# The first MLP as Strassen block products, with its middle rows kept in HBM

## The chip, the core and the metric

The kernel runs on one core of one Trainium2 chip. The metric is the device time of one launch in microseconds. The five engines of the core are TensorE (PE, with its weight loads listed as PEld), VectorE (DVE), ScalarE (ACT), GpSimd (POOL) and SyncE (SP), which here only issues transfers.

## The reference, cut to what matters

The model is a decoder trunk of two layers over 1040 tokens (16 meta tokens and 1024 others) of width 1024. Layer 0 mixes tokens by a recurrence and by attention, layer 1 by retention. After each mixer stands an MLP with a hidden width of 4096, and after each of the four parts a layer norm over a residual sum. The change is in the MLP of layer 0 and in what stands around it:

```
mix = _even_mixer(h, ...)                                  # ends in a projection by ev_w_out
h = _layernorm(DN_ALPHA * h + mix, ln_mix_g[l], ln_mix_b[l])
f = jnp.square(jax.nn.relu(h @ mlp_w1[l])) @ mlp_w2[l]      # 1024 -> 4096 -> 1024
h = _layernorm(DN_ALPHA * h + f, ln_mlp_g[l], ln_mlp_b[l])
```

## The kernel before, in words

**Layout and precision.** Everything is held transposed: 128 features on the partitions, tokens along the free dimension, so the width of 1024 is 8 tiles. To keep the precision of float32, each operand is split into a rounded part (`hi`, made by ACT, `round`, L294) and a remainder (`lo`, made by DVE's subtraction, L288 for weights). A product of two such pairs takes three matmuls per 128 rows of contraction (`mm3`, L321 to L323): hi x hi, hi x lo, lo x hi.

**Slots.** SBUF is cut into 50 slots of 1040 float32 per partition. `self.free` is a deque of their numbers: `slot` takes from its left end, `drop` puts back at its right end. The number is thus fixed while the program is written out. A tile in a slot that was used before waits for every reader and writer of the earlier tile, transfers among them. PSUM's eight banks of 512 float32 per partition are handed out in rings of their own (`bank`): s0 to s3 with one bank each, t0 and t1 with two.

**Weights.** `plan` lists all weight units of 128 x 1024 in the order of use. `weight` hands out the next one, and `ahead` loads and splits those that follow, as long as slots are free beyond a reserve.

**The MLP.** `out_proj` multiplies the attention half of the mixer's output, in four chunks of tokens (272, 256, 256, 256), and adds into the residual `acc` (L907). The norm of a chunk is a generator, `layer_norm`, put on a list; `pump` writes out a few of its steps between the matmuls of the next chunk, `settle` the rest. It sums over the tiles on POOL (L393, L395), subtracts the mean and scales on DVE (L406, L442), and splits the result (L449, L450); L452 keeps the residual. `mlp` then takes the hidden width in 8 blocks of 4 tiles. Up: one unit of w1 by all of x, then relu, square and split (L921 to L924). Down: four units of w2 by the block's four hidden tiles, added into `acc` by DVE (L956). The first block and the last run in the four chunks, so that they overlap with the norms before and after; all others run in three spans of 348, 346 and 346 columns. Hidden rows stay in SBUF.

**Order.** The order of the program gives the priority. A list scheduler that works with its own estimate of durations fixes the order on each engine and each queue when the program is built; on the chip each engine then goes through its list in order and waits where something isn't ready.

## Time and profile before

| | us |
|---|---|
| median of 3 runs (2863.98 to 2865.64) | 2864.4 |
| span of the profiled execution, from first to last instruction | 2862.4 |
| PE busy | 2795.6 (98%) |
| PE weight loads busy | 2531.5 (88%) |
| DVE busy | 1342.0 (47%) |
| ACT busy | 972.1 (34%) |
| POOL busy | 329.0 (11%) |

The profile gives for the profiled execution its span; nothing else of that execution's own time is shown, and the median of the timed runs lies 2.0 us above the span. Consecutive matmuls overlap in the profile, since each is shown with its whole passage through the array. The distance from start to start is therefore the cost of one, and PE's busy share says little of its pace. The granted clock is shown as a share of full speed.

### The profile page before, as it was taken

How to read it: one execution, taken by the hardware profiler on the slowest of the kernel's cores; microseconds unless marked ns; L12 is line 12 of the kernel's file. 1: busy time of each engine (PE TensorE's matmuls, PEld its weight loads, DVE VectorE, ACT ScalarE, POOL GpSimd, SP SyncE). 2: the span in 40 equal slices, each digit the busy share in tenths (PEclk: the TensorE clock that was granted, in tenths of full speed). 3: DMA queues.
4: the chain of work that ended last, by engine and by line, in shares of the span. 5: the costliest groups of instructions: out<-in, count | busy, mean ns of one | idle time of the engine just before them, and what ended most of it. 6: DMA issues, size and time to landing. Idle time of an engine off the chain costs nothing.

```text
span 2862.4 us, 38749 instructions
## 1 busy us (share of the span) xinstructions
PE 2795.6 (98%) x16142; PEld 2531.5 (88%) x16142; DVE 1342.0 (47%) x2381; ACT 972.1 (34%) x1857; POOL 329.0 (11%) x431
## 2 busy tenths in 40 slices
PE   8999999999999999989999999999999999999997
PEld 8898899999999999978888888788998888888896
DVE  6677868532233323575534635354473222222335
ACT  3757733522332223232414224141244212222133
POOL 1024524200000000230000000012140000000012
PEclk9999999999999999999999999999999999999998
DMA  3220130110111111111301303043101111111111
GB/s 135 74 72 5 53 134 16 38 59 30 52 37 60 41 49 45 45 45 52 125 16 45 118 35 114 15 140 125 67 31 38 59 52 37 52 40 56 52 37 60
DMA packets 49359, 168.53 MB, mean 59 GB/s; under 512 B 5776, under 2 KB 9616, under 8 KB 49184
## 3 DMA queue, kind: packets, MB, share of 16 engines
q1 hardware_dynamic: 40320, 134.97, 13.6%
q0 software_dynamic: 8288, 28.96, 3.1%
q8 instruction: 126, 2.06, 0.3%
q10 hardware_dynamic: 576, 2.13, 0.2%
q14 instruction: 49, 0.40, 0.0%
HBM read 143.94 MB, written 18.91 MB: 57 GB/s over the span
## 4 chain that ended last, share of the span: by engine, by line
PE 92%; DVE 4%; ACT 2%; issue 1%; POOL 1%; DMA 1%; POOLq 0%; SPq 0%; ACTq 0%; DVEq 0%
PE p L321 29%; PE p L323 29%; PE p L322 29%; PE p L847 1%; PE p L1266 1%; PE p L1267 1%; PE p L1268 1%; PE p L871 1%; DVE s L442 1%; DVE s L450 1%; PE p L873 1%; ACT s L825 0%; DVE s L406 0%; DVE st L818 0%; DMA s<-in_xT 0%
## 5 line engine op out<-in xcount | busy, mean ns | idle before, releaser
L321 PE MATMUL p<-s,s 128*128 128x512 f32 (+6 forms) x4886 | 1653.5, 340 | 28.2 <-POOL s L369 7.0
L322 PE MATMUL p<-s,s 128*128 128x512 f32 (+6 forms) x4886 | 1649.4, 338 | 1.5 <-DVE s L372 1.5
L323 PE MATMUL p<-s,s 128*128 128x512 f32 (+6 forms) x4886 | 1642.7, 338 | 1.6 <-DVE s L450 1.6
L321 PEld LDWEIGHTS p<-s,s 128*128 128x128 f32 (+1 forms) x4886 | 918.1, 188 | 113.3 <-ACT s L825 9.2
L322 PEld LDWEIGHTS p<-s,s 128*128 128x128 f32 (+1 forms) x4886 | 919.7, 188 | 77.4 <-DVE s L372 2.5
L323 PEld LDWEIGHTS p<-s,s 128*128 128x128 f32 (+1 forms) x4886 | 918.5, 188 | 77.5 <-DVE s L450 2.0
L294 ACT CAST s<-s 128x1024 fp32r<-128x1024 f32 (+5 forms) x331 | 277.4, 855 | 811.9 <-PE p L322 351.6
L956 DVE TENSOR_TENSOR s<-s,p 128x348 f32<-128x348 f32 (+4 forms) x328 | 178.7, 547 | 486.3 <-PE p L323 485.8
L288 DVE TENSOR_TENSOR s<-s,s 128x1024 fp32r<-128x1024 f32 x212 | 258.9, 1227 | 160.1 <-ACT s L294 103.0
L924 DVE TENSOR_TENSOR s<-s,s 128x346 fp32r<-128x346 f32 (+3 forms) x172 | 95.4, 563 | 337.8 <-ACT s L923 337.8
L921 ACT ACTIVATE s<-p 128x346 f32<-128x346 f32 (+3 forms) x172 | 82.7, 490 | 401.7 <-PE p L323 279.2
L393 POOL TENSOR_TENSOR s<-s,s 128x256 f32<-128x256 f32 (+1 forms) x16 | 13.9, 868 | 1383.3 <-DVE s L956 1262.6
L922 ACT ACTIVATE s<-s 128x346 f32<-128x346 f32 (+3 forms) x172 | 90.2, 525 | 3.2
L923 ACT CAST s<-s 128x346 fp32r<-128x346 f32 (+3 forms) x172 | 86.7, 513 | 3.9
L395 POOL TENSOR_TENSOR s<-s,s 128x256 f32<-128x256 f32 (+1 forms) x95 | 74.0, 781 | 104.9 <-DVE s L956 54.1
L1120 DVE TENSOR_TENSOR s<-p,s 128x512 fp32r<-128x512 f32 x32 | 22.1, 691 | 117.7 <-ACT s L1119 117.7
L341 DVE TENSOR_TENSOR s<-s,s 128x512 fp32r<-128x512 f32 (+6 forms) x121 | 65.1, 571 | 22.4 <-ACT s L294 20.7
L829 POOL TENSOR_SCALAR s<-s,st 116x808 f32<-116x808 f32 (+7 forms) x72 | 56.6, 789 | 79.0 <-DVE st L828 65.3
L850 DVE TENSOR_TENSOR s<-p,s 116x464 fp32r<-116x464 f32 (+3 forms) x120 | 59.3, 513 | 7.0 <-ACT s L849 5.6
L408 ACT ACTIVATE s<-s 128x256 f32<-128x256 f32 (+1 forms) x64 | 22.8, 417 | 115.0 <-DVE s L406 115.0
L1119 ACT CAST s<-p 128x512 fp32r<-128x512 f32 x32 | 18.7, 585 | 125.8 <-PE p L323 125.8
L847 PE MATMUL p<-consts,s 116*116 116x116 f32 (+2 forms) x360 | 54.7, 271 | 6.3 <-DVE s L850 1.9
(203 smaller groups left out, 1871.3 us busy)
## 6 DMA issues: line engine op xcount, KB each, us to landing
s<-in_w SPq DMA_DIRECT2D x128, 512.0 KB, 3.3
y_scratch<-s POOLq DMA_DIRECT2D x24, 512.0 KB, 9.3
s<-y_scratch POOLq DMA_DIRECT2D x24, 512.0 KB, 5.6
s<-in_wv SPq DMA_DIRECT2D x16, 512.0 KB, 4.2
s<-in_wg SPq DMA_DIRECT2D x16, 512.0 KB, 3.3
s<-in_xT SPq DMA_DIRECT2D x12, 520.0 KB, 5.6
s<-in_win SPq DMA_DIRECT2D x11, 512.0 KB, 8.7
s<-in_wout SPq DMA_DIRECT2D x8, 512.0 KB, 4.5
```

What stands on the lines that cost most here:

```text
L288: (self.nc.gpsimd if self.pool_lo else self.nc.vector).tensor_sub(lo[:, :n], s[:, :n], hi.f[:, :n])
L294: self.nc.scalar.copy(out, in_)
L321: self.nc.tensor.matmul(ps, wh, xh, start=(i == 0), stop=False)
L322: self.nc.tensor.matmul(ps, wh, xl, start=False, stop=False)
L323: self.nc.tensor.matmul(ps, wl, xh, start=False, stop=(stop and i == n - 1))
L395: (nc.vector if end and m == KT - 1 else nc.gpsimd).tensor_add(s1, s1, acc[m][:, cols])
L847: nc.tensor.transpose(tp[:n, c, :r], ps[q][:r, a:b], self.ident[:r, :r])
L921: nc.scalar.activation(r[:, lo:hi], ps, AF.Relu)
L922: nc.scalar.activation(r[:, lo:hi], r[:, lo:hi], AF.Square)
L923: nc.scalar.copy(h[0][:, lo:hi], r[:, lo:hi])
L924: nc.vector.tensor_sub(h[1][:, lo:hi], r[:, lo:hi], h[0].f[:, lo:hi])
L956: nc.vector.tensor_add(acc[m][:, lo:hi], acc[m][:, lo:hi], ps)
```

## The change

The product of w1 and x, and seven eighths of the product of w2 and the hidden rows, go by a scheme of Strassen's kind (in Winograd's form): both matrices are cut into 2 x 2 blocks, and the product is made of seven block products of sums of blocks, in place of eight products of blocks. The tokens are cut into four quads of 260, two to each half (q = 0, 1).

- `out_proj` runs in the quads. `norm_quad` normalises a quad, writes the result to HBM (`xd`) through POOL's queue, and after the second quad of a half forms four sums (two on DVE, two on POOL) and splits seven operands into hi and lo, 14 slots a half.
- A unit of the up half is a pair of w1 units (256 hidden rows). `make("w")` forms four sums and seven split operands of it in seven slots. `up` runs the seven products for two streams (two halves of the tokens). STEPS gives the order of the products, the PSUM accumulator each goes to (0, 1 or 2), and whether it begins a new sum there. A product that doesn't begin one adds to what the accumulator holds; after each product the accumulator's present value is read out (`evac`): by ACT copies or DVE adds into the stream's h.
- `finish` makes relu squared of h (DVE), forms four sums of the middle rows in t (POOL), and writes h and t to HBM (`hd`) by three transfers of POOL's queue. For the last 512 hidden rows (u = 14 and 15) there are no sums, and h goes to `hs`.
- The down half takes the middle rows back from HBM in blocks of 4, 4, 4 and 2 k-tiles a stream, splits them (`make("h")`), and adds each accumulator's values into `acc` on DVE, which has been reloaded from `xd`. The last 512 hidden rows go through the plain product in the four old chunks, with the norm behind it as before.
- The preparation is a list of work, `queue_up`, in which each piece is fetched two items ahead of its making. `feed` writes out up to four steps of it after each product and stops where too few slots are free; `need` writes out what must be there.

The program of the retention layer and the second MLP is left as it is. The diff, cut:

```diff
+QUADS = [(0, 260), (260, 520), (520, 780), (780, 1040)]
+BLOCKS = [4, 4, 4, 2]
+STEPS = [(0, 0, True), (1, 1, True), (5, 0, False), (4, 2, True), (6, 0, False), (2, 2, False), (3, 0, False)]
+FEED = 4
...
-            y, acc = self.even_mixer(x)
-            x, acc = self.mlp(0, y, acc, T, SPANS, CHUNKS, keep=False)
+            acc = self.even_mixer(x)
+            x, acc = self.smlp(acc)
...
+            if l == 0:
+                o = [u for b in w1 for u in b]
+                for b in range(len(BLOCKS)):
+                    o += [d[f"w2s_{b}"][m] for m in range(KT)]
+                self.pairs = (len(u), len(u) + len(o))
+                return o + [d["w2_0"][i] for i in range(4)]
...
-        end = len(self.units)
+        end = len(self.units) if self.n_used >= self.pairs[1] else self.pairs[0]
...
+        if emit:
+            mean = var = self.bank("l")[:, :w]
+        else:
+            st = self.bank("t")
...
+            if emit:
+                nc.scalar.activation(emit(m), a, AF.Identity, bias=b[:, m:m + 1])
+                yield True
+                continue
...
+    def norm_quad(self, acc, c, g, b):
+        nc, (lo, hi) = self.nc, QUADS[c]
+        n = hi - lo
+        q, half = c // 2, c % 2
+        raws = [self.slot(F32, (P, 4, n)) for _ in range(2)]
+        yield from self.layer_norm(acc, lo, hi, g, b, None, False, emit=lambda m: raws[m // 4][:, m % 4, :])
+        for h in range(2):
+            nc.gpsimd.dma_start(self.xd[4 * h:4 * h + 4, :, lo:hi].rearrange("j p t -> p j t"), raws[h][:, :, :])
+        yield True
+        self.half = self.half + raws if half else raws
+        if c == 3:
+            self.drop(*acc)
+        if half:
+            b11, b21, b12, b22 = self.half
+            t1, t2 = self.slot(F32, (P, 4, n)), self.slot(F32, (P, 4, n))
+            nc.vector.tensor_sub(t1[:, :, :], b12[:, :, :], b11[:, :, :])
+            nc.vector.tensor_sub(t2[:, :, :], b22[:, :, :], t1[:, :, :])
+            yield True
+            t3, t4 = self.slot(F32, (P, 4, n)), self.slot(F32, (P, 4, n))
+            nc.gpsimd.tensor_sub(t3[:, :, :], b22[:, :, :], b12[:, :, :])
+            self.drop(b12)
+            nc.gpsimd.tensor_sub(t4[:, :, :], b21[:, :, :], t2[:, :, :])
+            yield True
+            ops = [b11, b21, b22, t4, t1, t2, t3]
+            for p, _, _ in STEPS:
+                r = ops[p]
+                h, l = self.slot(F32R, (P, 4, n)), self.slot(F32R, (P, 4, n))
+                self.round(h.t, r.t)
+                yield True
+                nc.vector.tensor_sub(l.t, r.t, h.f)
+                yield True
+                self.drop(r)
+                ops[p] = (h, l)
+            self.xo[q] = ops

+    def queue_up(self):
+        self.xo, self.half, self.work, self.made, self.ops = [None, None], None, deque(), set(), {}
+        items = [("w", u) for u in range(16)]
+        for b, n in enumerate(BLOCKS):
+            for m in range(4):
+                items.append(("w", 16 + 4 * b + m))
+                if m == 0:
+                    items += [("h", b, p) for p, _, _ in STEPS]
+        items += [x for i in range(4) for x in (("v", i), ("r", i))]
+        ahead = 2
+        for k in range(-ahead, len(items)):
+            if k >= 0:
+                self.work.append((items[k], self.make(*items[k])))
+            if k + ahead < len(items):
+                self.work.append((None, self.fetch(*items[k + ahead])))
+
+    def take(self, n, got, dt=F32, shape=(P, 1024)):
+        while len(self.free) < n + self.reserve:
+            yield False
+        got += [self.slot(dt, shape) for _ in range(n)]
...
+    def pieces(self, raw, got, shape=(P, 1024)):
+        yield from self.take(2, got, F32R, shape)
+        h, l = got[-2:]
+        self.round(h.t, raw.t)
+        yield True
...
+    def fetch(self, kind, i, p=0):
...
+            for _ in range(2):
+                while len(self.free) < 1 + self.reserve:
+                    yield False
+                self._load()
...
+            n, raws = BLOCKS[i], []
+            if n == 4:
+                yield from self.take(2, raws, F32, (P, n, 260))
+                for q in range(2):
+                    nc.sync.dma_start(raws[q].t, self.hd[i][q, p])
...
+    def make(self, kind, i, p=0):
...
+            (r0, _), (r1, _) = self.raw.pop(self.n_ready), self.raw.pop(self.n_ready + 1)
+            tmp = []
+            yield from self.take(1, tmp, F32, (P, n))
+            s12 = tmp[0]
+            nc.vector.tensor_add(s12[:, a], r1[:, a], r1[:, b])
+            nc.vector.tensor_sub(s12[:, b], s12[:, a], r0[:, a])
+            yield True
+            yield from self.take(1, tmp, F32, (P, n))
+            s34 = tmp[1]
+            nc.gpsimd.tensor_sub(s34[:, a], r0[:, a], r1[:, a])
+            nc.gpsimd.tensor_sub(s34[:, b], r0[:, b], s12[:, b])
+            yield True
+            yield from self.take(1, got, F32R, (P, n))
+            h3 = got[0]
+            self.round(h3[:, a], r1[:, b])
+            nc.vector.tensor_sub(h3[:, b], r1[:, b], h3.f[:, a])
+            self.drop(r1)
+            yield True
+            for s in (s12, _Slot(r0.t[:, :n], r0.i), s34):
+                yield from self.pieces(s, got, (P, n))
+            h3, h12, l12, h0, l0, h34, l34 = got
+            w = [(h0[:, a], l0[:, a]), (h0[:, b], l0[:, b]), (h34[:, b], l34[:, b]), (h3[:, a], h3[:, b]),
+                 (h12[:, a], l12[:, a]), (h12[:, b], l12[:, b]), (h34[:, a], l34[:, a])]
+            self.ops["w", i] = (w, {1: (h0, l0), 4: (h12, l12), 2: (h34, l34), 3: (h3,)})
...
+            for r in self.ops["raw", i, p]:
+                yield from self.pieces(r, got, (P, n, 260) if n == 4 else (P, 2, n, 260))
+                h, l = got[-2:]
+                out += [(h.t, l.t)] if n == 4 else [(h[:, q], l[:, q]) for q in range(2)]
...
+    def feed(self, n, key=None):
+        while self.work and (n > 0 or key not in self.made | {None}):
+            k, gen = self.work[0]
+            got = next(gen, None)
+            if got is None:
+                self.work.popleft()
+                self.made.add(k)
+            elif got is False:
+                assert n > 0, (key, k, len(self.free))
+                return
+            n -= 1
...
+    def products(self, streams, evac, used, early=False, pump=0):
+        nc = self.nc
+        n = 260
+        a = self.bank("t0" if early else "t")
+        b = [self.bank(f"s{i}") for i in range(2)]
+        chains = [[a[:, i, :n] for i in range(2)], [x[:, :n] for x in b], None]
+        for p, ch, start in STEPS:
+            if ch == 2 and start:
+                c = self.bank("t1") if early else None
+                chains[2] = [c[:, i, :n] for i in range(2)] if early else [self.bank(f"s{i + 2}")[:, :n] for i in range(2)]
+            for i, (w, x) in enumerate(streams):
+                ps = chains[ch][i]
+                (wh, wl), (xh, xl) = w[p], x(p)
+                nk, skip = xh.shape[1], not start
+                for k in range(nk):
+                    c = slice(P * k, P * k + P)
+                    nc.tensor.matmul(ps, wh[:, c], xh[:, k, :], start=(start and k == 0), stop=False, skip_group_check=skip)
+                    nc.tensor.matmul(ps, wh[:, c], xl[:, k, :], start=False, stop=False, skip_group_check=skip)
+                    nc.tensor.matmul(ps, wl[:, c], xh[:, k, :], start=False, stop=(k == nk - 1), skip_group_check=skip)
+                evac(i, p, ps)
+            used(p)
+            if p == 3 and self.reserve:
+                self.reserve = max(self.reserve, 3)
+            self.feed(FEED)
+            self.pump(pump)

+    def up(self, streams, last, early=False, pump=0):
+        nc = self.nc
+        hs = [self.slot(F32, (P, 4, 260)) for _ in streams]
+        self.reserve = 1
+        if early:
+            self.reserve = 0
+        for u, q in streams:
+            self.need("w", u)
+        self.reserve = 14 if early else 1
+
+        def x_of(q):
+            return lambda p: (self.xo[q][p][0][:, :, :], self.xo[q][p][1][:, :, :])
+
+        def evac(i, p, ps):
+            h = hs[i]
+            if p in (0, 5, 4, 3):
+                nc.scalar.copy(h[:, {0: 0, 5: 1, 4: 3, 3: 2}[p], :], ps)
+            else:
+                d = h[:, {1: 0, 6: 3, 2: 1}[p], :]
+                nc.vector.tensor_add(d, d, ps)
+            if p == 3:
+                finish(i, *streams[i])
+
+        def finish(i, u, q):
+            h = hs[i]
+            nc.vector.scalar_tensor_tensor(h[:, :, :], h[:, :, :], 0.0, h[:, :, :], ALU.max, ALU.mult)
+            if u >= 14:
+                for r in range(2):
+                    nc.gpsimd.dma_start(self.hs[2 * u - 28 + r][:, 520 * q:520 * q + 520], h[:, 2 * r:2 * r + 2, :])
+            else:
+                b, k = u // 4, u % 4
+                t = self.slot(F32, (P, 4, 260))
+                nc.gpsimd.tensor_sub(t[:, 1:4:2, :], h[:, 1:4:2, :], h[:, 0:2, :])
+                nc.gpsimd.tensor_sub(t[:, 2, :], h[:, 3, :], t[:, 1, :])
+                nc.gpsimd.tensor_sub(t[:, 0, :], h[:, 2, :], t[:, 2, :])
+                d = self.hd[b][q, :, :, k, :].rearrange("o p t -> p o t")
+                nc.gpsimd.dma_start(d[:, 0:1, :], h[:, 0:1, :])
+                nc.gpsimd.dma_start(d[:, 1:3, :], h[:, 2:4, :])
+                nc.gpsimd.dma_start(d[:, 3:7, :], t[:, :, :])
+                self.drop(t)
+            self.drop(h)
+
+        ws = [self.ops["w", u] for u, _ in streams]
+
+        def used(p):
+            if last:
+                for k in {u for u, _ in streams}:
+                    self.drop(*self.ops["w", k][1].get(p, ()))
+            if streams[0][0] == 15:
+                for q in range(2):
+                    self.drop(*self.xo[q][p])
+
+        self.products([(w[0], x_of(q)) for w, (_, q) in zip(ws, streams)], evac, used, early, pump)

+    def smlp(self, acc):
+        nc = self.nc
+        self.up([(0, 0), (1, 0)], False, True, PN)
+        self.settle()
+        self.up([(0, 1), (1, 1)], True)
+        for u in range(2, 16):
+            self.up([(u, 0), (u, 1)], True)
+        self.reserve = 0
+        acc = []
+        for m in range(KT):
+            t = self.slot()
+            nc.sync.dma_start(t[:, :], self.xd[m])
+            acc.append(t)
+        for b, n in enumerate(BLOCKS):
+            for mp in range(4):
+                self.need("w", 16 + 4 * b + mp)
+                w, slots = self.ops["w", 16 + 4 * b + mp]
+
+                def x_of(q):
+                    def get(p):
+                        self.need("h", b, p)
+                        return self.ops[b, p][0][q]
+                    return get
+
+                def evac(i, p, ps):
+                    row, half, first = {0: (0, 0, True), 1: (0, 0, False), 5: (0, 1, True), 4: (1, 1, True),
+                                        6: (1, 1, False), 2: (0, 1, False), 3: (1, 0, True)}[p]
+                    lo = 260 * (2 * i + half)
+                    d = acc[2 * mp + row][:, lo:lo + 260]
+                    if first and b == 0:
+                        nc.vector.scalar_tensor_tensor(d, d, ALPHA, ps, ALU.mult, ALU.add)
+                    else:
+                        nc.vector.tensor_add(d, d, ps)
+
+                def used(p):
+                    self.drop(*slots.get(p, ()))
+                    if mp == 3:
+                        self.drop(*self.ops[b, p][1])
+
+                self.products([(w, x_of(q)) for q in range(2)], evac, used)
...
+        ws = [self.weight(reserve=18, splits=6 - m) for m in range(4)]
+        x = [(self.slot(F32R), self.slot(F32R)) for _ in range(KT)]
...
-        x = y + [(self.slot(F32R), self.slot(F32R)) for _ in range(4)]
-        for lo, hi in CHUNKS:
+        self.queue_up()
+        for c, (lo, hi) in enumerate(QUADS):
             for m in range(KT):
-                ps = self.bank("all")[:, :hi - lo]
+                ps = self.bank("w")
+                ps = (ps[:, 0, :] if len(ps.shape) == 3 else ps)[:, :hi - lo]
                 self.gemm(ps, ws[m // 2], y, lo, hi, k0=4 * (m % 2))
                 nc.vector.tensor_add(acc[m][:, lo:hi], acc[m][:, lo:hi], ps)
                 self.pump(PG)
             if hi == T:
-                for w in ws:
+                for w in ws + y:
                     self.drop(*w)
             self.settle()
-            self.later(lo, self.layer_norm(acc, lo, hi, self.g00, self.b00, x, True))
-        return x, acc
+            self.later(lo, self.norm_quad(acc, c, self.g00, self.b00))
+        return acc
```

## Rows read from the trace of the kernel before

**Rows 1.** The page: its head, and the chain that ended last, by engine.
```profile
span 2862.4 us, 38749 instructions
...
PE 92%; DVE 4%; ACT 2%; issue 1%; POOL 1%; DMA 1%; POOLq 0%; SPq 0%; ACTq 0%; DVEq 0%
```

**Rows 2.** Windows: stretch, length, busy us (instructions) of each engine, clock, DMA share, GB/s.
```profile
431.76:534.35 102.59, 97.94 (x778) 96.05 (x777) 84.24 (x191) 47.79 (x119) 46.60 (x60) 0.98 0.05 20
534.35:1177.66 643.31, 643.04 (x4058) 642.75 (x4057) 194.52 (x310) 169.28 (x309) 0.00 (x0) 1.00 0.13 46
1177.66:1229.00 51.34, 46.73 (x369) 46.32 (x367) 41.96 (x83) 15.28 (x31) 23.60 (x24) 0.93 0.14 51
```

**Rows 3.** Windows of 10 us around the norms behind out_proj.
```profile
440.00:450.00 10.00, 10.00 (x84) 9.92 (x83) 4.92 (x14) 1.78 (x5) 3.05 (x4) 1.00 0.01 2
...
460.00:470.00 10.00, 10.00 (x86) 10.00 (x86) 10.00 (x24) 5.96 (x14) 4.03 (x5) 1.00 0.00 0
```

**Rows 4.** Timeline of PE: start, duration; first and last of two unbroken runs.
```profile
433.01 0.29 PE L322 MATMUL p<-s,s 128*128 128x272 f32 x1
...
435.90 0.29 PE L321 MATMUL p<-s,s 128*128 128x272 f32 x1
...
2759.82 0.28 PE L321 MATMUL p<-s,s 128*128 128x256 f32 x1
...
2762.91 0.28 PE L323 MATMUL p<-s,s 128*128 128x256 f32 x1
```

**Rows 5.** Groups by line and shape: busy us, mean ns, idle time before them.
```profile
L288 DVE TENSOR_TENSOR s<-s,s 128x1024 fp32r<-128x1024 f32 x212 | 258.9, 1227 | 160.1 <-ACT s L294 103.0 <-PE p L322 48.7 <-POOL s L285 4.3
...
L341 DVE TENSOR_TENSOR s<-s,s 128x512 fp32r<-128x512 f32 x48 | 30.3, 688 | 0.6
...
L341 DVE TENSOR_TENSOR s<-s,s 128x1040 fp32r<-128x1040 f32 x4 | 5.0, 1243 | 5.3 <-ACT s L294 5.3
...
L406 DVE TENSOR_TENSOR s<-s,p 128x256 f32<-128x256 f32 x112 | 38.7, 415 | 3.3 <-PE p L399 3.3
...
L450 DVE SCALAR_TENSOR_TENSOR s<-s,params,s 128x256 fp32r<-128x256 f32 x80 | 41.2, 575 | 0.0
...
L924 DVE TENSOR_TENSOR s<-s,s 128x256 fp32r<-128x256 f32 x28 | 12.3, 450 | 15.7 <-ACT s L923 15.7
...
L921 ACT ACTIVATE s<-p 128x256 f32<-128x256 f32 x28 | 10.3, 379 | 15.9 <-PE p L323 15.8
...
L395 POOL TENSOR_TENSOR s<-s,s 128x256 f32<-128x256 f32 x83 | 64.7, 782 | 100.1 <-DVE s L956 54.1 <-DVE s L1087 31.1 <-DVE s L907 12.6
...
L1289 POOL TENSOR_TENSOR s<-s,s 128x1024 f32<-128x1024 f32 x4 | 9.6, 2408 | 222.1 <-ACT s L1287 222.1
...
L1060 POOL DMA_DIRECT2D y_scratch<-s x24 | 12.9, 542 | 113.9 <-ACT s L294 112.1 <-DVE s L341 1.8
```

**Rows 6.** Timelines of DVE and of POOL, 481 to 487.
```profile
483.26 0.95 DVE L416 TENSOR_TENSOR s<-s,s 128x256 f32<-128x256 f32 x1
...
486.45 0.42 DVE L416 TENSOR_TENSOR s<-s 128x256 f32<-128x256 f32 x1 [0.48 <-ACT s L412]
...
481.24 5.31 POOL L395 TENSOR_TENSOR s<-s,s 128x256 f32<-128x256 f32 x6
```

**Rows 7.** Line 1060, POOL's writes of 512 KB to y_scratch: issue to landing.
```profile
DMA to landing us min/median/max: 5.4/9.3/13.5
```

**Rows 8.** Tile r_scratch, SP's transfers of 520 KB: issue to landing.
```profile
DMA to landing us min/median/max: 2.6/3.2/4.5
```

**Rows 9.** Timelines of POOL and ACT, in brackets the idle time before and its releaser.
```profile
1770.41 0.53 POOL L1060 DMA_DIRECT2D y_scratch<-s  x1 [0.60 <-DVE s L341]
...
1780.09 1.81 ACT L294 CAST s<-s 128x1024 fp32r<-128x1024 f32 x3 [5.90 <-DMA y_scratch<-s]
```

**Rows 10.** Timeline of PE in the last block: first and last of 21 starts.
```profile
1222.56 0.58 PE L321 MATMUL p<-s,s 128*128 128x256 f32 x1 [4.61 <-DVE s L956]
...
1226.99 0.39 PE L323 MATMUL p<-s,s 128*128 128x256 f32 x1
```

More of the change, by code (lines that the diff above doesn't have):

```diff
@@ L165, in f, with r, __init__ @@
         return self.t.bitcast(F32)
+    @property
+    def r(self):
+        return self.t.bitcast(F32R)
 class _Trunk:
[L169 removed]
+    def __init__(self, tc, d, out, scratch, spill, xd, hd, hs):
+        self.xd, self.hd, self.hs = xd, hd, hs
         self.tc, self.nc, self.d, self.out, self.scratch, self.spill = tc, tc.nc, d, out, scratch, spill
@@ L384, in rstd, with layer_norm @@
         return y
-    def layer_norm(self, acc, lo, hi, g, b, x, keep, out=None):
+    def layer_norm(self, acc, lo, hi, g, b, x, keep, out=None, emit=None):
         nc = self.nc
```

75 lines of the change are left out of this document (70 added, 5 removed).

## Prediction

> **What bounds the kernel now.** I read the page first, then the windows by stage, then single lines. The page gives a span of 2862.4 us and a chain that runs 92% of the time through PE [rows 1], so a matmul saved is time saved unless something else is late. The median of the timed runs is 2864.4, 2.0 more than the span; I work out a difference in the profiled execution and add it to that median. Three stretches matter [rows 2]: out_proj's second half with the MLP's first block (102.59 us), the rest of the MLP up to its last block (643.31 us), and that last block (51.34 us). The reader is to see that PE is without a gap in the second, where DVE works 194.5 us of 643, ACT 169 and POOL nothing at all; and that the first has DVE at 84.2 of 102.6, in places full [rows 3].
>
> **The matmuls.** In the first two stretches, 745.90 us, stand 384 matmuls of out_proj, 384 of the first block and 4032 at 346 or 348 columns (28 up units and 28 down units of 72). The change keeps the 384 of out_proj, now 260 wide, and puts 5040 in place of the 4416: 16 up units x 2 token halves x 7 products x 4 k-tiles x 3, which is 2688 in 32 lots of 84, and down 3 blocks of 672 and one of 336. The last block's 384 stay. No matmul of 260 is in the trace. At 272 columns 24 starts lie 2.89 us apart from first to last, 125.7 ns each, at 256 columns 27 starts 3.09 us, 118.9 ns [rows 4]; a quarter of the way between them gives 120.6 ns. So the pace still follows the columns here, and the weight loads, one per matmul, set no floor above it. 5424 x 0.1206 = 654.1 us against 745.90: **91.8 us less if nothing waits**. That is the most the change can bring.
>
> **Vector, Scalar and GpSimd work.** For one pair of w1 units, DVE has three two-input operations of 512 columns and three of 1024, 3 x 0.69 + 3 x 1.23 = 5.8 us; per token half three adds from PSUM at 0.42 and one of 1040 at 1.24, together 5.0 for two halves [rows 5]. That is 10.8 us beside 168 x 0.1206 = 20.3 us of PE. POOL has 1024 columns for the weights (2.4 us) and 2 x 1040 for the sums of the middle rows (2 x 2.8), ACT some 7 us. None of the three fills the set. In the down half a set of 20.3 us has 14 adds (5.9), 5.8 for weights and a quarter of 14 splits (4.3), 16.0 us on DVE: hidden on the mean, but at each change of block all 14 splits fall into about two sets, 40.6 us with 11.8 + 11.6 + 17.4 = 40.8 of work. I take 3 us lost at each of the three changes, 8 us for the last block, whose sets are half as long (10.1 us of PE against about 11 of DVE) and which has eight more splits of 1.2 behind it, and 2 for the reload of the residual: 19 us, bounds 0 and 40.
>
> **The start.** The first product now needs both quads of a half normalised, combined and split, where before a chunk sufficed. From the 84.2 us of DVE work go the 32 of L450 (0.575, 18.4 us), the 16 of L924 (0.45, 7.2) and three splits (3.7); until the second half's first product come 11.5 for two weight pairs, 5.0 for four sums, 9.9 for eight splits and 5.0 for the first set's results: 84.2 - 29.3 + 31.4 = 86.3 us. DVE is about half idle until 450 and full from there [rows 3], so it is through between 518 and 529, depending on how much weight work goes ahead of 450. PE has 552 matmuls, 66.6 us from 431.76, ending at 498.3. I take 25 us of waiting plus 2 for the clock (below). Bounds: 10, if the operations overlap as the back-to-back ones do, and 45, if the 28 POOL adds of 0.78 us block DVE: at 483 to 486 a DVE add of two SBUF tiles takes 0.95 us instead of 0.42 while POOL adds run back to back [rows 6]. The Trainium skill (SBUF — State Buffer, "SBUF: two separate sides") has a DVE operation with two SBUF inputs and a reading GpSimd operation exclude each other for their whole length; those rows agree, and by it alone the start would be near the upper bound, 20 us later.
>
> **The h slots, the term that decides.** SBUF is 50 slots, handed out first freed, first taken. I followed that order by hand through a steady up set. At its head 28 slots hold x, 2 the set's h, 14 the pieces of this weight pair and the next, 4 raw weights, 1 a sum: 49. Four steps of `feed` follow each product and take what is freed. After the sixth product three are free: two of this pair's pieces and a scratch. At the end stream 0 takes the first for its t and returns t and h, stream 1 the second, and the last product returns one more: scratch, t0, h0, t1, h1, piece. The reserve of 3 lets `feed` take three (two loads and a sum), so the next set's h are **the slots of t1 and h1**, whose contents are just then on their way to HBM. The first copy out of PSUM of the next set must wait for that transfer to land, and the third product, which adds into the same PSUM bank, waits for that copy.
>
> When does t1 land? Count from the set's last matmul. Stream 0 was done 1.45 us before; ACT copy 0.38, DVE square 1.24 and some 0.3 for hand-overs: 0.5. Three POOL subtractions, 1.22 + 0.78 + 0.78: 3.3. Three DMA issues at 0.54 [rows 5]: 4.9. Stream 1's subtractions: 7.7; its third issue starts at 8.8. A POOL write of 512 KB landed 5.4 us after issue at best, 9.3 in the median where eight were queued [rows 7]; an SP transfer of 520 KB took 2.6 at best, 3.2 in the median [rows 8]. I take 5.4: 14.2, with the copy 14.7. PE needs it after four streams of 1.45 us, at 5.8. **PE waits 8.9 us in the set.** That a write holds up the next user of a slot is in the trace: ACT waited 5.9 us until 1780.09 for a transfer issued at 1770.41 [rows 9]. And an idle PE comes back slow: after 4.61 us without work, 21 matmuls of 256 columns start 4.43 us from first to last, 0.22 apart where 0.119 is usual, the 1.2 GHz level [rows 10]; that is 2.0 us more. So 10.9 us in each of the 13 sets u = 2 to 14 whose predecessor wrote t: 142 us. Set 15 follows one with no t and waits about 0.
>
> Bounds of this term. Below: stream 1's subtractions directly behind stream 0's (6.0), one issue, 2.6 to land, copy: 9.7, a wait of 3.9, no clock loss, 51 us in all. Above: the issue costs 0.54 per 128 pieces (seven per stream, 3.8 us) and the landing takes 9.3: 13.6 + 9.3 - 0.5, 22.9 with the copy, a wait of 17.1 and 2.0 for the clock, 248 us. I take the middle way because three issues and a best landing are the nearest rows. By the fit in the Trainium skill (DMA: Bandwidth & Descriptors, "Anatomy of one DMA — SWDGE (gpsimd) path"), 2.0 us and 436 GB/s, t1 would land in an estimated 3.2 us, the wait would be 6.7 and the total 29 us lower; no row has a single POOL write to test it.
>
> **Sum.** 654.1 + 27 + 142 + 19 = 842.1 against 745.9: 96 us more, 2864.4 + 96 = **2960 us**. The retention layer and the second MLP are as before.
>
> **Rivals.**
> (1) Faster: the slots are free in time. Then 654.1 + 27 + 19 = 700.1, 45.8 us less: 2819. It decides where t1 has landed 5.3 us after a set ends, 9 us sooner than I have it; for it speaks that the planner may order POOL's work better and that I count durations where operations overlap, against it that POOL's subtractions alone last to 6.0.
> (2) Slower still: POOL's issue time grows with the pieces of 1040 bytes. 654.1 + 27 + 248 + 19 = 948, 3067 us. For it: the 0.54 us of L1060 are for whole rows of 4 KB, so the piece is untried; against it: even seven times as many pieces would have to be paid in full, with none of the issue's 0.54 us fixed.
> (3) The narrow matmul doesn't pay: at 0.1585 us as for 346 columns, 5040 cost 191 us more, 3150. The pace of the narrow matmuls [rows 4] speaks plainly against it.
>
> **How the numbers follow.** Forecast 0.70, with its own range 2900 to 3030 (start 10 to 45, wait 4 to 13 with its clock cost, down 0 to 40); rival 1 0.21, of which 0.02 end within 0.2%; rival 2 0.08; rival 3 0.01. A tail of 0.04 of the forecast's, towards the lower bounds all together (654.1 + 10 + 51 + 0 = 715, 31 us less), is not slower either: 0.03 faster, 0.01 the same. 0.2%, 5.7 us, is what a measurement can tell from no change. So slower 0.75, same 0.03, faster 0.22. The range 2815 to 3045 leaves out half of rival 1 and most of rival 2.
>
> **What would show it.** Right: in every up set from u = 2 on PE idles after four streams, about 9 us, released by ACT's copy, and ACT by an `h_scratch` transfer; a set lasts about 31 us instead of 20.3; the granted clock of the up half is near 0.9; down sets last 20.3 us. Wrong: up sets of 20 to 22 us, or DVE as the releaser of most of PE's idle time. The start is right if the second half's first product is issued between 510 and 545.

## The result, and the profile after

The changed kernel takes **3131.4 us** in the median (3123.0 to 3133.8, 4 runs) against 2865.0 beside it: a ratio of 1.092, 95% interval 1.091 to 1.094. I had said 2960, range 2815 to 3045: the right sign, in the main the forecast's mechanism, and a cost 2.8 times too small (96 us against 266). The page, beside [rows 1]:

```profile
span 3128.5 us, 41046 instructions
PE 2803.7 (90%) x16766; PEld 2511.1 (80%) x16766; DVE 1575.9 (50%) x2637; ACT 1005.5 (32%) x1820; POOL 543.5 (17%) x650
...
PEclk9999996888788899999899999999999999999998
...
PE 66%; POOL 3%; DMA 3%; DVE 3%; issue 3%; ACT 1%; POOLq 0%; DVEq 0%; ACTq 0%; SPq 0%
```

PE's share of the span falls from 98 to 90%, its share of the chain from 92 to 66%, and links of POOL and DMA appear. I divide the stretch at its products, counted in order of time: the 337th of 5040 (the first two up units are through), the 2689th (up half through), the last. The windows between these (stretch, length, busy us of PE, PEld, DVE, ACT, POOL, clock, DMA share, GB/s), beside [rows 2]:

```profile
431.80:588.36 156.56, 102.59 (x707) 96.70 (x706) 114.14 (x189) 58.17 (x110) 66.32 (x60) 0.77 0.21 73
588.36:1116.32 527.96, 345.10 (x2354) 328.76 (x2353) 173.36 (x202) 97.05 (x176) 157.04 (x187) 0.82 0.27 90
1116.32:1446.76 330.44, 310.64 (x2496) 304.88 (x2495) 238.24 (x381) 103.37 (x114) 48.68 (x41) 0.98 0.39 130
```

| stretch | matmuls at 0.1206 | loss predicted | loss measured |
|---|---|---|---|
| start: out_proj's half and units 0, 1 | 86.8 | 27 | 69.8 |
| up, 14 sets | 283.6 | 142 | 244.3 |
| down, and the difference after it | 283.6 | 19 | 43.8 (46.8 - 3.0) |

The three differences are 43, 102 and 25 us, together the 170 by which the span missed. An up set lasts 527.96 / 14 = 37.7 us in the mean, not 31. Who waits for whom in the up half (total, times, longest):

```profile
PE p L767 <- ACT s L793: 175.6, 55, 9.1
...
ACT s L793 <- POOL s L811: 119.8, 13, 10.4
...
ACT s L793 <- DMA h_scratch<-s: 78.9, 13, 7.5
```

That is the place of the prediction: PE waits for ACT's copy out of PSUM (L793), and ACT waits 13 times for GpSimd's last reading of h1 (L811) and 13 times for the write of t1. The prediction had the write alone; there are two long waits in a set, and the longer one ends with GpSimd's reading. One set, timelines of PE, ACT and POOL (start, duration, in brackets the idle time before and its releaser):

```profile
709.00 0.28 PE L769 MATMUL p<-s,s 128*128 128x260 f32 x1
709.75 0.39 PE L767 MATMUL p<-s,s 128*128 128x260 f32 x1 [0.47 <-ACT s L793]
...
719.27 0.59 PE L767 MATMUL p<-s,s 128*128 128x260 f32 x1 [7.83 <-ACT s L793]
719.66 0.42 PE L768 MATMUL p<-s,s 128*128 128x260 f32 x1
719.88 0.42 PE L769 MATMUL p<-s,s 128*128 128x260 f32 x1
...
726.93 0.58 PE L767 MATMUL p<-s,s 128*128 128x260 f32 x1 [4.69 <-ACT s L793]
```
```profile
718.85 0.38 ACT L793 COPY s<-p 128x260 f32<-128x260 f32 x1 [9.15 <-POOL s L811]
726.50 0.66 ACT L793 COPY s<-p 128x260 f32<-128x260 f32 x2 [7.28 <-DMA h_scratch<-s]
```
```profile
708.96 1.28 POOL L809 TENSOR_TENSOR s<-s 128x520 f32<-128x520 f32 x1 [27.03 <-DVE s L802]
...
711.49 1.27 POOL L700 TENSOR_TENSOR s<-s,s 128x512 f32<-128x512 f32 x1
...
717.28 0.77 POOL L815 DMA_DIRECT2D h_scratch<-s  x1
718.07 0.74 POOL L811 TENSOR_TENSOR s<-s,s 128x260 f32<-128x260 f32 x1
719.45 1.27 POOL L701 TENSOR_TENSOR s<-s,s 128x512 f32<-128x512 f32 x1 [0.64 <-DVE s L696]
720.66 0.77 POOL L815 DMA_DIRECT2D h_scratch<-s  x1
```

The set's last matmul (709.00) ends at 709.28; t1's write is issued at 720.66 and lands at about 726.45: 17.2 us after the set's end, not 14.2. The copy at 726.50 empties an accumulator whose stream PE had run ahead at 670, a whole set earlier. Both token halves' first accumulators are the two halves of one PSUM tile (`bank("t")`, 2 x 512), and in the program as built the second half's stream on it waits for the copy of the first half's. So at 726.93 PE begins a row of seven streams on this tile, each of which waits for the read-out of the one before, with the other streams between them; the last matmul of the row starts at 747.6, and only then the next finish can begin. From start to start the loop is 17.9 + 20.7 = 38.6 us. Between the set's last matmul and 726.93 PE has two streams of other accumulators (709.75 and 719.27); nothing of the next set's work on that tile covers the write.

### The profile page after: what moved, and what is told of

It reads as the page before. It is cut to its first block, busy times and chain, and to the rows that moved or that the text cites. A ratio compares the mean times of both kernels' runs of the same rounds, so it can differ in the third digit from the quotient of the medians.

```text
span 3128.5 us, 41046 instructions
## 1 busy us (share of the span) xinstructions
PE 2803.7 (90%) x16766; PEld 2511.1 (80%) x16766; DVE 1575.9 (50%) x2637; ACT 1005.5 (32%) x1820; POOL 543.5 (17%) x650
## 4 chain that ended last, share of the span: by engine, by line
PE 66%; POOL 3%; DMA 3%; DVE 3%; issue 3%; ACT 1%; POOLq 0%; DVEq 0%; ACTq 0%; SPq 0%
PE p L345 16%; PE p L343 16%; PE p L344 16%; PE p L767 5%; PE p L769 4%; PE p L768 4%; DMA h_scratch<-s 2%; DVE s L656 1%; PE p L1592 1%; PE p L1593 1%; PE p L1594 1%; POOL s L809 1%; DMA s<-in_w2s 1%; POOL s L811 1%; POOL s L810 1%
## 5 line engine op out<-in xcount | busy, mean ns | idle before, releaser
L343 PE MATMUL p<-s,s 128*128 128x512 f32 (+7 forms) x3414 | 1187.5, 350 | 30.7 <-ACT s L478 8.3
L344 PE MATMUL p<-s,s 128*128 128x512 f32 (+8 forms) x3414 | 1183.1, 347 | 2.0 <-DVE s L394 2.0
L345 PE MATMUL p<-s,s 128*128 128x512 f32 (+8 forms) x3414 | 1177.6, 347 | 3.2 <-DVE s L479 3.2
L343 PEld LDWEIGHTS p<-s,s 128*128 128x128 f32 (+2 forms) x3414 | 641.6, 188 | 115.8 <-ACT s L1150 9.6
L767 PE MATMUL p<-s,s 128*128 128x260 f32 x1680 | 508.1, 306 | 230.4 <-ACT s L793 187.2
L345 PEld LDWEIGHTS p<-s,s 128*128 128x128 f32 (+1 forms) x3414 | 641.8, 188 | 80.2 <-DVE s L479 4.7
L344 PEld LDWEIGHTS p<-s,s 128*128 128x128 f32 (+2 forms) x3414 | 642.4, 188 | 78.2 <-DVE s L394 2.9
L316 ACT CAST s<-s 128x1024 fp32r<-128x1024 f32 (+6 forms) x466 | 397.0, 872 | 866.8 <-PE p L344 163.3
L767 PEld LDWEIGHTS p<-s,s 128*128 128x128 f32 x1680 | 340.7, 204 | 253.5 <-ACT s L793 200.8
L768 PE MATMUL p<-s,s 128*128 128x260 f32 x1680 | 497.4, 298 | 9.1 <-DVE s L656 8.2
L769 PE MATMUL p<-s,s 128*128 128x260 f32 x1680 | 489.5, 297 | 6.1 <-DVE s L656 6.1
L768 PEld LDWEIGHTS p<-s,s 128*128 128x128 f32 x1680 | 343.6, 205 | 10.7 <-DVE s L656 9.4
L769 PEld LDWEIGHTS p<-s,s 128*128 128x128 f32 x1680 | 338.8, 204 | 8.3 <-DVE s L656 8.3
L656 DVE TENSOR_TENSOR s<-s,s 128x1024 fp32r<-128x1024 f32 (+2 forms) x149 | 185.6, 1253 | 93.6 <-ACT s L316 80.4
L1282 DVE TENSOR_TENSOR s<-s,p 128x512 f32<-128x512 f32 (+1 forms) x128 | 79.5, 621 | 254.6 <-PE p L345 254.2
L793 ACT COPY s<-p 128x260 f32<-128x260 f32 x128 | 46.4, 375 | 357.0 <-PE p L769 146.5
L796 DVE TENSOR_TENSOR s<-s,p 128x260 f32<-128x260 f32 x96 | 40.5, 421 | 141.3 <-ACT s L793 114.7
L863 DVE TENSOR_TENSOR s<-s,p 128x260 f32<-128x260 f32 x192 | 77.1, 420 | 37.9 <-PE p L769 36.9
```

The source lines that it names most:

```text
L316: self.nc.scalar.copy(out, in_)
L343: self.nc.tensor.matmul(ps, wh, xh, start=(i == 0), stop=False)
L344: self.nc.tensor.matmul(ps, wh, xl, start=False, stop=False)
L345: self.nc.tensor.matmul(ps, wl, xh, start=False, stop=(stop and i == n - 1))
L656: self.nc.vector.tensor_sub(l.t, raw.t, h.f)
L767: nc.tensor.matmul(ps, wh[:, c], xh[:, k, :], start=(start and k == 0), stop=False, skip_group_check=skip)
```

## Experiments

The kernel before took 2864.99, 2864.16, 2863.57 and 2864.63 us in the four series, in which each of these kernels was timed. Theory A is the loop through the slot.

**1. The slots.** Slots being written are kept back until the next set's third product, and the planner leaves four free for it, so that a set's h lies in slots that only TensorE has read.

```diff
-            if p == 3 and self.reserve:
-                self.reserve = max(self.reserve, 3)
+            if p == 2 and self.reserve:
+                self.reserve = max(self.reserve, 4)
+            if p == 5:
+                self.drop(*self.wet)
+                self.wet = []
...
-                self.drop(t)
+                self.wet += [t, h]
+                return
```

> Only the order in which buffer slots are handed out in the up half is changed: slots being written to HBM are kept back until the third product of the next set, so a set's two h slots are slots that only TensorE has read. Theory A (the loop through the slot: h slot written out late, next set's first PSUM copy waits for it): the 7.8 and 4.7 us gaps per set go, an up set falls from 38.6 us to 21-23, 13 sets give back 200-230 us: 2900-2935. Rival B (both streams' first accumulators are one PSUM tile, so its eight streams and their read-outs run one after another): 8 x (1.45 + 0.5 copy + 0.2) = 17 us stand in a line, with stalls of 0.5 us left on most of them and a clock that stays low: a set of 25-30 us, 2980-3050. Rival C (POOL's subtractions and its DMA issue are the pace, whatever slot is used): no change, 3100-3135.

Measured: **2879.5** (ratio to before 1.0047, 1.0031 to 1.0063). 252 us back, more than A's range.

**2. The tiles.** Each of a set's six accumulators gets a PSUM tile of its own.

```diff
-        a = self.bank("t0" if early else "t")
-        b = [self.bank(f"s{i}") for i in range(2)]
-        chains = [[a[:, i, :n] for i in range(2)], [x[:, :n] for x in b], None]
+        if early:
...
+        else:
+            chains = [[self.bank(f"s{i}")[:, :n] for i in range(2)],
+                      [self.bank(f"s{i + 2}")[:, :n] for i in range(2)], None]
...
-                chains[2] = [c[:, i, :n] for i in range(2)] if early else [self.bank(f"s{i + 2}")[:, :n] for i in range(2)]
+                chains[2] = [c[:, i, :n] for i in range(2)] if early else [self.bank(f"t{i}")[:, 0, :n] for i in range(2)]
```

> Only the PSUM tiles of the MLP's later sets are changed: each of the six accumulators of a set is a tile of its own, so no stream waits for the read-out of the other stream's accumulator. Slots as in the changed kernel. Theory A with its waits as predicted (four streams of cover, 5.8 us, before the slot is needed): the set falls from 38.6 to about 30-32 us, 13 x 7 = 90 us back: 3030-3050. Rival B (the shared tile is the cause): 21-24 us per set, 2910-2950. Rival D (the order of the tiles plays no part): 3120-3135.

Measured: **2939.2** (1.0253, 1.0236 to 1.0270), in rival B's range, not in A's. One set of it, copies of ACT and the one wait of PE (the lines are of two views):

```profile
700.84 0.65 ACT L795 COPY s<-p 128x260 f32<-128x260 f32 x2 [2.09 <-POOL s L813]
701.27 0.39 PE L769 MATMUL p<-s,s 128*128 128x260 f32 x1 [2.44 <-ACT s L795]
...
706.42 0.66 ACT L795 COPY s<-p 128x260 f32<-128x260 f32 x2 [2.30 <-DMA h_scratch<-s]
```

PE waits for the copy 13 times, 40.5 us in all, each time behind a copy that GpSimd's last reading released, as at 701.27. ACT still waits for the write, but no wait of PE follows: with the tiles apart the write is covered, and GpSimd's reading of the old h is not quite. The edit also changed the built order: t1 is here the first of the two to be written (issued at 702.66), and more than six streams stand between a set's end and the one that needs the copy at 706.42.

**3. Both.**

> Both edits together: slots being written are kept back, and each accumulator is a tile of its own. Theory A and rival B agree: an up set is 20.3-21.5 us, and what is left over the kernel before is the start (some 60 us lost) and the down half (some 30): 2865 + 62 + 30 - 92 + 10 = 2875, range 2855-2905. Rival C (POOL's pace): over 3050.

Measured: **2869.1** (1.0009, 0.9999 to 1.0018), level with the kernel before. Windows of the up half in the three, first slots, then tiles, then both:

```profile
574.58:868.47 293.89, 286.80 (x2355) 284.54 (x2353) 169.80 (x201) 94.69 (x176) 176.32 (x187) 0.99 0.46 160
```
```profile
587.14:942.56 355.42, 311.78 (x2355) 308.64 (x2354) 175.49 (x204) 94.79 (x175) 164.04 (x188) 0.91 0.38 134
```
```profile
574.13:864.85 290.72, 284.99 (x2355) 284.50 (x2354) 177.74 (x205) 99.45 (x178) 177.11 (x188) 0.99 0.45 155
...
600.00:650.00 50.00, 50.00 (x420) 50.00 (x418) 30.12 (x33) 15.59 (x30) 33.06 (x36) 1.00 0.38 127
```

Per set that is 21.0, 25.4 and 20.8 us against 37.7. The gains don't add up: the slots alone give 252 us, the tiles alone 192, both 262. Without the late slot the shared tile costs 0.2 us a set; without the shared tile the late slot costs 4.6; together they cost 16.9, since the shared tile takes away the cover. With both gone PE has hardly a gap, DVE works 178 us of 291 and POOL 177: rival C (POOL's pace) is out.

**4. Is it the loop? Its length, both ways,** each one edit on the changed kernel alone. First the weight sums, which stand in POOL's queue inside the chain, on VectorE; then a second write of t, behind the first.

```diff
-            nc.gpsimd.tensor_sub(s34[:, a], r0[:, a], r1[:, a])
-            nc.gpsimd.tensor_sub(s34[:, b], r0[:, b], s12[:, b])
+            e = nc.vector if i < 16 else nc.gpsimd
+            e.tensor_sub(s34[:, a], r0[:, a], r1[:, a])
+            e.tensor_sub(s34[:, b], r0[:, b], s12[:, b])
```
```diff
-                nc.gpsimd.dma_start(d[:, 3:7, :], t[:, :, :])
+                for _ in range(2):
+                    nc.gpsimd.dma_start(d[:, 3:7, :], t[:, :, :])
```

> One edit on the changed kernel alone, slots and tiles as they are there: the weight sums (two subtractions of 512 columns per pair) are made by VectorE, not by GpSimd, where in the trace they stand between a set's subtractions and its transfers (1.27 us twice, 2.5 of the 17.2 us from the set's last matmul to the landing of t1). Loop theory: the up half's period is that chain, so 2.5 us less in it are 2 to 2.5 us less per set, 13 sets: 26 to 33 us, 3098-3105, although VectorE gets 2.5 us more work per set. Rival (the two shared PSUM accumulators and VectorE's share set the period): no change or slower, 3128-3150.

> One edit on the changed kernel alone: each set's t is written to HBM twice, the second write waiting for the first, so that t1's slot comes free later by one issue (0.77) and one landing (4.5 to 5.8 us). Loop theory: 5 to 6.5 us more per set, 13 sets: 65 to 85 us, 3196-3216. Rival (the transfer is beside the path, the period is TensorE's serial accumulators): under 15 us, 3131-3146.

Measured: **3081.6** and **3163.6**, 50 us less and 32 more. Both lie on the loop theory's side and outside its ranges, the first beyond, the second short, and outside those of the rivals. A set of each, POOL's first subtraction, its last issue, and ACT's copy, shorter chain first (the lines are of two views, timelines of POOL and ACT):

```profile
695.72 1.28 POOL L810 TENSOR_TENSOR s<-s 128x520 f32<-128x520 f32 x1 [23.75 <-DVE s L803]
...
705.50 0.77 POOL L816 DMA_DIRECT2D h_scratch<-s  x1 [0.30 <-POOL s L812]
...
709.30 0.65 ACT L794 COPY s<-p 128x260 f32<-128x260 f32 x2 [3.69 <-DMA h_scratch<-s]
```
```profile
718.11 1.28 POOL L809 TENSOR_TENSOR s<-s 128x520 f32<-128x520 f32 x1 [24.37 <-DVE s L802]
...
733.51 0.75 POOL L816 DMA_DIRECT2D h_scratch<-s  x1 [2.19 <-DMA h_scratch<-s]
...
737.35 0.65 ACT L793 COPY s<-p 128x260 f32<-128x260 f32 x2 [8.99 <-DMA h_scratch<-s]
```

From the first subtraction to the copy it is 13.6, 17.5 (the changed kernel, above) and 19.2 us; the period of a set, the mean of 14, is 34.6, 37.7 and 39.7. The period goes with the chain in both directions, 3.1 us down for 4.0 and 2.0 up for 1.7, although VectorE has more work per set in the first: the loop theory holds, its rivals don't. My prices of the edits were off. The second write came 3.7 us behind the first and was followed by the copy after 3.8, where in the set shown of the changed kernel it was 5.8, so the slot was late by 1.7, not by 5 to 6.5. In the first the 2.5 us brought 4.0 in this set: the last issue came 9.8 us after the first subtraction instead of 11.7, and the landing took 3.8 instead of 5.8 (see the last section).

**5. The start,** on top of 3: the first weight pair loaded and made during out_proj's second quad; or the norm's sum over the row tiles by TensorE for two quads; or both, with the first two operands split right after the first quad.

```diff
+            if c == 1:
...
+                self.need("w", 0)
```
```diff
+        if onpe:
+            for m in range(KT):
+                nc.tensor.matmul(mean, self.ones, acc[m][:, cols], start=(m == 0), stop=(m == KT - 1))
```
```diff
+        if c == 0:
+            self.pre = []
+            for r in raws:
...
+                nc.vector.tensor_sub(l.t, r.t, h.f)
```

> On top of the slot and tile edits: the seven pieces of the first weight pair are loaded and made while out_proj's second quad runs (from about 408 us on, when SyncE is idle and VectorE half idle), not after out_proj has given its slots back at 476. Theory S (the first products wait for the weight pair, whose load is issued at 476 and whose split is done at 495): the first product starts near 487 instead of 494.6, about 6 us of VectorE and 2.4 of GpSimd leave the crowded stretch, 8 to 14 us back of the 2869: 2855-2861. Rival T (norm and split of the token quads on VectorE and GpSimd set the start, weights or not): less than 4 us, 2865-2870.

> On top of the slot and tile edits: for the third and fourth quad the sum over the eight row tiles that the norm's mean needs is made by TensorE (eight matmuls with the ones, accumulated) instead of seven chained GpSimd adds. Theory T (GpSimd's adds, stretched from 0.78 to 1.0-1.7 us beside VectorE, hold up the norm for which TensorE waited 10.5 us at 509-520, and stretch VectorE's splits from 1.25 to 2.1): 8 to 16 us back, 2853-2861. Rival S (weights hold up the start): under 4 us, 2865-2870.

> Slot and tile edits, early first weight pair, sums on TensorE for two quads, and the first two operands of the first half split right after its first quad. If the start costs about 50 us as the gaps of the trace say (18 + 11 + 5 + 4 + 2 + 3 + 6 and slow matmuls between them) and these three reach the first three gaps: 20 to 32 us back, 2837-2849, faster than the kernel before. If VectorE's total work from 476 to 575 is the limit whatever comes first: 10 us back, 2857-2862.

Measured: **2862.8**, **2854.8**, **2853.1**: 6, 14 and 16 us less than 3. Theory T hits; the early weights bring less than S said and more than T, though the first product comes at 475. The three together lie between the two ranges put down for them, 20 to 32 and about 10. What they free is probably in part the same, which wasn't tried by itself: VectorE is busy 24.6 and 24.2 us of each 25 from 475 to 525. Against before the last has a ratio of 0.9964 (0.9951 to 0.9977).

**6. What is left of the start,** on top of that. The first four pairs' subtractions by VectorE; with it the two sums per token half by VectorE; or with it eight steps of `feed` per product in the last two up sets.

```diff
+            e = nc.vector if i < 4 else nc.gpsimd
+            e.tensor_sub(s34[:, a], r0[:, a], r1[:, a])
+            e.tensor_sub(s34[:, b], r0[:, b], s12[:, b])
```
```diff
-            nc.gpsimd.tensor_sub(t3[:, :, :], b22[:, :, :], b12[:, :, :])
+            nc.vector.tensor_sub(t3[:, :, :], b22[:, :, :], b12[:, :, :])
...
-            nc.gpsimd.tensor_sub(t4[:, :, :], b21[:, :, :], t2[:, :, :])
+            nc.vector.tensor_sub(t4[:, :, :], b21[:, :, :], t2[:, :, :])
```
```diff
+        self.fd = 8 if streams[0][0] >= 14 else FEED
```

> The fastest version so far (slots, tiles, early first pair, sums on TensorE, early split) with one more edit: for the first four weight pairs GpSimd's two subtractions of 512 columns are made by VectorE. Theory P (the 7.0 us stall at 559-566, in which GpSimd is busy 23.2 us of 25 and VectorE 11.5, is GpSimd's queue: its sums and DMA issues of four streams stand ahead of the third pair's subtractions): that stall goes, VectorE has 2.8 us more per pair, 4 to 8 us back of 2853: 2845-2850. Rival V (VectorE is the limit in the start as a whole): no gain or up to 5 us slower, 2852-2858.

> As e3_weights, and the two sums of 1040 columns per token half that GpSimd makes (3.4 to 3.9 us each in the start, 1.25 where nothing runs beside it) are made by VectorE. Theory X (GpSimd and VectorE take turns on SBUF, so VectorE's split of 1040 takes 2.09 us beside GpSimd instead of 1.25): VectorE's stretched splits shorten by about what the added sums cost, 4 x 1.25: within 3 us of e3_weights, and the split's mean in the start falls to below 1.6. Rival Y (they run side by side, and the long times are waits for something else): 5 us slower than e3_weights, the mean unchanged.

> As e3_weights, and in the up half's last two sets the planner takes eight steps of feed per product instead of four. Theory F (the change from the up to the down half loses about 10 us because the middle rows' loads and splits are put out too late in the order): the stretch 850-900 loses under 4 us, 5 to 8 us back against e3_weights. Rival M (they wait for slots that only the last set's products give back, whatever the order): within 2 us of e3_weights.

Measured: **2846.7** (0.9939, 0.9924 to 0.9954), 2848.4 and 2848.1. The first is the fastest version found and beats both kernels. Its time is in theory P's range, but the stall doesn't go: PE's longest wait from 550 to 575 falls from 6.7 to 4.2 us. The second comes out as theory X says, within 3 us, and not as Y. VectorE's split of 1040 from 476 to 575 in the first and in the second version (busy, mean ns):

```profile
L643 DVE TENSOR_TENSOR s<-s,s 128x1040 fp32r<-128x1040 f32 x12 | 18.0, 1520 | 1.1 <-ACT s L316 1.1
```
```profile
L643 DVE TENSOR_TENSOR s<-s,s 128x1040 fp32r<-128x1040 f32 x12 | 14.5, 1231 | 0.1
```

Without POOL's sums beside it the split takes its 1.23 us, and the time stays level: what VectorE takes over it gets back. That the mean is below 1.6 says little, since it was so before this edit. The third moves the stall at the change to the down half, and doesn't shorten it (PE is idle 4.5 us of these 50 in the first, 7.8 in the third; windows of the first, then of the third):

```profile
840.00:865.00 25.00, 24.22 (x199) 23.80 (x198) 18.73 (x27) 10.68 (x13) 3.03 (x5) 1.00 1.03 411
865.00:890.00 25.00, 21.29 (x161) 20.60 (x161) 17.89 (x26) 7.46 (x8) 4.22 (x4) 0.93 0.27 91
```
```profile
840.00:865.00 25.00, 17.23 (x138) 17.03 (x137) 18.05 (x24) 11.53 (x14) 4.64 (x6) 0.91 0.91 351
865.00:890.00 25.00, 25.00 (x202) 25.00 (x202) 15.08 (x25) 4.82 (x5) 2.79 (x2) 0.96 0.25 94
```

That agrees with rival M, slots that only the last set's products give back; what holds them wasn't tried by itself.

## Why the prediction was right and wrong

**The matmuls: right.** 420 starts in 50.00 us of the version with both edits are 0.119 us each; I took 0.1206 [rows 4]. Rival 3 is out. So the 91.8 us are there, and some 8 more; what the change loses it loses in waits and at the slow pace.

**Work beside PE: right** for the steady sets: hidden, with DVE at 178 us of 291, 12.7 a set for my 10.8, and POOL at 177, its issuing of transfers among it.

**The h slots: right place, wrong cover.** The slots are those of t1 and h1; PE waits for ACT's copy, ACT for the transfer, 13 times; and the set without its late slot lasts 21. The step that failed is "PE needs it after four streams of 1.45 us, at 5.8". I took the two token halves as independent, while `products` asks for one tile (`bank("t")`) for both: the copy that waits releases not the third product but the other half's first, and all that follows. In the set shown two streams cover the late slot and not four, and PE idles 7.83 + 4.69 = 12.5 us, not 8.9; 30 starts at the slow pace cost 3.0, not 2.0; and two read-outs of the row add waits of 0.5. The landing came 3.0 us later than worked out. POOL's two weight subtractions (1.27 each), which the order as built put ahead of the transfers, I had left out of the queue although I counted them as work; without them the issue came 1.9 us sooner (experiment 4). 10.9 became 37.7 - 20.3 = 17.4. With the tiles apart the cover is longer than the four streams I gave it (more than six): the second version loses 25.4 - 20.3 = 5.1 a set, and there PE waits for GpSimd's reading of h1 and never for the write. GpSimd's reading, which also holds h1's slot, stands in my sum only as work ahead of the write, not as a wait of its own.

**The landing: right size, by luck.** 5.8 us after issue in the set shown, 4.1 in the next, against 5.4 [rows 7]. My 5.4 is the best of the writes of [rows 7], several of which stood in the queue together; here a weight load runs beside the write (last section), and the median of the 28 writes of 520 KB is 3.4. By the fit in the Trainium skill (DMA: Bandwidth & Descriptors, "Anatomy of one DMA — SWDGE (gpsimd) path") I had an estimated 3.2. The median agrees with it; most of the writes that decide, 5.2 to 6.2 us in the changed kernel, come later than it says. Rival 2 is out: the issue takes 0.57, 0.71 and 0.77 us for one, two and four rows of 260 per partition, where it had 0.54 for each row. That its 3067 lay nearer than my 2960 is luck.

**The start: too cheap, 69.8 for 27.** My sign that it is right, the second half's first product between 510 and 545, came true (544.0), and yet the stretch lost 43 us more: that product ran ahead of its turn, and the half's p0 came at 571.4. Windows, then timelines of SP and ACT in the changed kernel:

```profile
475.00:500.00 25.00, 4.62 (x22) 3.60 (x20) 23.07 (x23) 10.91 (x17) 17.10 (x10) 0.57 0.42 153
500.00:525.00 25.00, 9.64 (x42) 7.37 (x42) 23.34 (x37) 9.40 (x20) 14.89 (x13) 0.64 0.01 4
```
```profile
473.01 23.08 SPq L289 DMA_DIRECT2D s<-in_w  x6
```
```profile
482.50 2.02 ACT L316 CAST s<-s 128x1040 fp32r<-128x1040 f32 x2
...
492.90 2.01 ACT L316 CAST s<-s 128x1024 fp32r<-128x1024 f32 x2 [4.82 <-DMA s<-in_w]
```

Experiments 1 to 6 take it apart: 14 us belong to the slots (337th product at 588.4, with the slots alone 574.6, with both 574.1); 19 more go by the four edits of 5 and 6 (555.2); 37 remain, with VectorE nearly full until 525 (24.4 and 23.9 of each 25 us from 475). Named causes: the first weights are loaded only from 473 on, since the program asks for them only behind out_proj and `ahead` no longer covers them (I had them made in part before 450); and POOL's sums beside VectorE, my upper bound of 45, which I named and did not take. Where the sums stand matters less than that there are so many: on VectorE they cost what they free. My rows for the upper bound show one side only: beside the same POOL adds, which run from 481.24 to 486.55, the same line of DVE took 0.41 us as well.

```profile
482.03 0.41 DVE L416 TENSOR_TENSOR s<-s,s 128x256 f32<-128x256 f32 x1
```

The rule of the Trainium skill (SBUF — State Buffer, "SBUF: two separate sides"), that such operations exclude each other, fits the two splits of 1520 and 1231 ns; the value by it, some 47, was nearer than mine. No run here tells exclusion from a mere slowing.

**The down half and what follows: too cheap, 43.8 for 19.** The version with both edits has 304.9 us for 283.6, a loss of 21.3, and from its last product to the end of the span 1696.3 against 1684.7 before, 11.6 more: 32.9 for the 19 that I gave to all of it. The changes of block, my 9 us, cost next to nothing (rows of the three stretches of that version):

```profile
864.85:900.00 35.15, 29.55 (x215) 28.54 (x214) 26.17 (x36) 12.36 (x15) 7.25 (x8) 0.90 0.67 265
900.00:1100.00 200.00, 199.85 (x1667) 199.55 (x1666) 145.30 (x228) 66.74 (x70) 29.15 (x20) 1.00 0.34 123
1100.00:1169.79 69.79, 66.67 (x528) 64.14 (x527) 59.42 (x111) 25.23 (x31) 6.26 (x7) 1.00 0.50 167
```

215 matmuls take 25.6 of the first 35.15: 9.5 us go at the change from up to down, which I had at nothing. The last 528 take 62.8 of 69.79: 7.0 us lost, near my 8 for the short block. The windows by themselves mislead, since they hold matmuls of the plain product behind too, some 140 in the changed kernel and some 50 here (x2496 and x2410 for 2352); so the loss is taken with what follows. With the tiles alone it is 29.5, with the slots alone 34.1. The 11.6 us behind the last product were not taken apart.

**The rivals.** Rival 1, the slots free in time, is what the versions 1 and 3 build: 2879 and 2869, not 2819. Even where it held the change was not faster: in version 3 the start costs 28.5 us more than I gave it (55.5 for 27), the down half and what follows 13.9 more, and the up half 7.1 where I had nothing, 50 in all. A chance of 0.22 for faster was too much.

## What to carry to other kernels

Where buffers are handed out in the order in which they come free, follow who still reads or writes the next one: a buffer that a slow engine still reads, or that is on its way to HBM, belongs behind those that only the fast engine has read. Cover is only what doesn't itself depend on the late event: follow the waits of the built program from that event on, and count two accumulators in one PSUM tile as one. A loop's period is the work behind the event plus its latency; lengthen and shorten the latency to see it.

## What was not expected of the hardware

After 7.83 us without work PE's next stream of 12 starts 0.215 us apart; after 4.69 us the slow pace lasts from 726.93 to about 730.9, and 0.119 comes back. The granted clock is 0.50 in both slow stretches (719.27 to 722.20 and 726.93 to 730.90), the 1.2 GHz level, and 1.00 from 731. In the up half this is a granted clock of 0.82 in the mean, against 0.99 with both edits; I had said near 0.9.

The write of the same 520 KB was followed by the copy after 3.8 to 5.8 us from its issue. The packets of the DMA queues during three writes (POOL's queue is q0, SP's loads go by q1; packets, MB, share of 16 engines) show what differs. First the write at 717.28, which landed after 3.4 us, then that at 720.66, after 5.8, both of the changed kernel, then that at 705.50 of the version with the shorter chain, after 3.8:

```profile
q0 software_dynamic: 151, 0.53, 44.6%
```
```profile
q1 hardware_dynamic: 144, 0.52, 36.8%
q0 software_dynamic: 144, 0.53, 23.2%
```
```profile
q0 software_dynamic: 244, 0.88, 68.5%
q1 hardware_dynamic: 46, 0.19, 22.3%
```

Of the changed kernel's 28 such writes 16 had no load beside them and landed after 3.4 us, 11 had a whole load of 512 KB beside them and landed after 5.2 to 6.2, and one, with half a load, after 4.1. So the landing goes with the weight load that runs beside the write; no run moved the loads by themselves.
